# Two early weight sums in DRAM instead of one, and one subtraction instead of two, in a seven-product step of a down projection

## The chip, the core and the metric

The kernel runs on one core of one Trainium2 chip. The metric is device time in microseconds (us) of one execution, as the median of several runs. The core has five engines that matter here: TensorE (matmul; PE in the profile, with its weight loads as PEld), VectorE (DVE), ScalarE (ACT), GpSimd (POOL) and SyncE (SP), which only issues transfers. Sixteen DMA engines move the data. Transfers are put on queues by SyncE, GpSimd and, rarely, ScalarE; each of these engines works through its own instructions in order, so a transfer that has to wait holds the instructions behind it on that engine.

## What is computed

One layer of a hybrid decoder on 272 tokens (16 of them prepended and dropped at the end): a mixed retention and mLSTM part, and then a gated feed-forward part with a causal convolution. Only the last part is touched by the change:

```python
h = h + mix
u = rmsnorm(h, norm_ffn)
up = causal_dwconv(u @ w_up, ffn_conv_w, ffn_conv_b)      # 2048 -> 2 x 5632
gate, val = jnp.split(up, [FFN_DIM], axis=-1)
h = h + (jax.nn.silu(gate) * val) @ w_down                # 5632 -> 2048
...
h = rmsnorm(h, norm_final)
```

All inputs are float32. The kernel multiplies with float32 accuracy on a faster, shorter type: each operand x is split into hi, x rounded to that type (a copy on ScalarE), and lo = x - hi (a subtraction on VectorE), and each product is the sum of three matmuls, hi*hi, hi*lo and lo*hi.

## The kernel before

**Stages.** The input projection and the two kinds of heads run first, then the output projection. The feed-forward part then runs in two halves over the 5632 inner columns (`for half in range(2)`, line 724). Each half has an up projection (22 inner tiles, two products each, lines 749 to 790) and a down projection for its inner columns (lines 897 to 938).

**The down projection of a half.** The output's 2048 columns are four blocks of 512, taken in pairs: b = 0 with 1, then b = 2 with 3. For each pair the half's 22 inner tiles are taken two at a time, in 11 steps q. A *plain* step (q in PLAIN: 0, 4, 9, 10) loads the weights of block b and of block b + 1 with `load_w` (line 115) and multiplies all of its 2 x 2 x 2 tiles: eight products. A *fast* step (q in FAST: 1, 2, 3, 5, 6, 7, 8) treats its two inner tiles, two row tiles and two column blocks as a 2 x 2 by 2 x 2 product of tiles, and computes it with seven products instead of eight, after Strassen and Winograd: some products take sums of left tiles (S1 to S4, made on GpSimd in lines 782 to 785) and sums of weight tiles. The function `seven` (line 812) does one such step. In the very last pair the fast steps 7 and 8 are plain, so there are 7 + 7 + 7 + 5 = 26 fast steps in all.

**The weights of a fast step.** Four weight tiles, 128 x 512 each: B11, B12, B21 and B22, where the first index is the inner tile within the step and the second the column block within the pair. Their order in DRAM is fixed on the host in `a["wd7"]` (line 1007): B12, B11, B22, B21. The seven products need B11, B22, B21 as they are and four sums:

- t1 = B11 - B12, t2 = B22 + t1, t2 - B11 and B21 - t2.

**The early sum.** t2 is made ahead of time, during the up projection. An `Early` object (line 704) loads three tiles of a unit into a borrowed buffer (`home`) on GpSimd's queue (line 715), two projections later forms t2 there with two 128x512 operations on VectorE (lines 720 and 721), and stores t2 to a DRAM tile `kept` on GpSimd's queue (line 722). In the first half the homes of the first nine units are `x5[1:4]`; the last five use `left[0]`, `left[1]`, `x5[1:4]`, `left[0]`, `left[1]` in this order. `left[0]` and `left[1]` are also the two buffers into which the fast steps load their weights in turn.

**A fast step in `seven`.** SyncE loads t2 from `kept` (line 820, 256 KB) and B11, B22, B21 (line 821, 768 KB) into `raw`, one of the two `left` buffers. VectorE forms ta = t2 - (B11, B22), two tiles at once, of which the second is t1 again (line 824), and tb = B21 - t2, one tile (line 825). ta and tb lie in slots of the ring `wraw`, which has four slots of two tiles and also takes the weights that `load_w` loads: a later load waits until the slot's last reader is done. Then four groups of weights, three of two tiles and one of one, are split with `split` (line 743: a ScalarE copy in line 744, a VectorE subtraction in line 746) into the rings `whi` and `wlo` of five slots each, and multiplied (lines 839, 840 and 842).

**Order.** The instructions are written in the order of the loops; a planner puts them into each engine's queue by a timeline that it simulates. The trace shows the order that came of it.

Of the kernel before, what the change touches and what calls it, by code (L numbers as in the profile page):

```python
# [10 lines left out]
F32 = mybir.dt.float32  # L11
# [5 lines left out]
P = 128  # L17
# [66 lines left out]
def trunk(ctx: ExitStack, tc: tile.TileContext, io, out: bass.AP):  # L84
# [619 lines left out]
    class Early:  # L704


        def __init__(self, b, q, home, after):

            self.home, self.age = home, 0
            self.kept = dram.tile([P, 512], F32, name=f"kept{b}_{q % NQD}", bufs=1)  # L710

            if after is not None:
                after = nc.gpsimd.tensor_tensor(out=pace, in0=after[:, 0:1], in1=after[:, 0:1], op=ALU.add)
            with tc.issue_after(after.ins) if after else nullcontext():
                nc.gpsimd.dma_start(home, io["wd7"][b // 2, q][:, 0:3, :])

        def finish(self, after):
            t = self.home[:, 0, :]
            with tc.issue_after(after.ins):
                nc.vector.tensor_tensor(out=t, in0=self.home[:, 1, :], in1=t, op=ALU.subtract)  # L720
            nc.vector.tensor_tensor(out=t, in0=self.home[:, 2, :], in1=t, op=ALU.add)
            nc.gpsimd.dma_start(self.kept, t)

    for half in range(2):
        units = [(b, q) for b in (0, 2) for q in FAST if (half, b) != (1, 2) or q not in BOTH]
# [23 lines left out]
        for jj in range(NHF):  # L749
# [20 lines left out]
            if q in PLAIN:  # L770
                k = 2 * PLAIN.index(q) + i
                copied, parted = split(mh[:, k, :], ml[:, k, :], gt)
            elif i == 0:
                f = FAST.index(q)
                even = gt
                copied, parted = split(sh[:, f, A11, :], sl[:, f, A11, :], gt[:, 0:P])
            else:
                e11, e21, e12, e22 = even[:, 0:P], even[:, P:], gt[:, 0:P], gt[:, P:]
                if half == 1 and q in BOTH:
                    split(*(a[:, BOTH.index(q), :] for a in a21), e21)  # L780
                sums = x_tile(0).rearrange("p (a t) -> p a t", a=4)
                nc.gpsimd.tensor_tensor(out=sums[:, S1, :], in0=e21, in1=e22, op=ALU.add)
                nc.gpsimd.tensor_tensor(out=sums[:, S3, :], in0=e11, in1=e21, op=ALU.subtract)
                nc.gpsimd.tensor_tensor(out=sums[:, S2, :], in0=sums[:, S1, :], in1=e11, op=ALU.subtract)
                nc.gpsimd.tensor_tensor(out=sums[:, S4, :], in0=e12, in1=sums[:, S2, :], op=ALU.subtract)
                split(sh[:, f, A12:, :], sl[:, f, A12:, :], gt.rearrange("p (a t) -> p a t", a=2))
                copied, parted = split(sh[:, f, 0:4, :], sl[:, f, 0:4, :], sums)
# [24 lines left out]
        def seven(b, q, cs, ps, first, last, after, norm):  # L812
# [4 lines left out]
            raw = left[turn]  # L817
            turn = 1 - turn

            nc.sync.dma_start(raw[:, 0, :], early[b, q])  # L820
            nc.sync.dma_start(raw[:, 1:4, :], io["wd7"][b // 2, half * NQD + q][:, 1:4, :])
            ta, tb = (wpool.tile([P, 2, 512], F32, name="wraw", bufs=4) for _ in range(2))

            nc.vector.tensor_tensor(out=ta, in0=raw[:, 0:1, :].to_broadcast([P, 2, 512]), in1=raw[:, 1:3, :], op=ALU.subtract)  # L824
            nc.vector.tensor_tensor(out=tb[:, 0, :], in0=raw[:, 3, :], in1=raw[:, 0, :], op=ALU.subtract)
            copied = None
            for w, to in (
                (raw[:, 2:4, :], ((S4, cs[0, 1], False, False), (A12, cs[0, 0], False, False))),
                (raw[:, 0:2, :], ((S2, ps[2], first, last), (A11, ps[0], first, last))),
                (ta, ((S3, ps[1], first, last), (S1, ps[3], first, last))),  # L830
                (tb[:, 0:1, :], ((A22, cs[1, 0], False, False),)),
            ):
                hi = wpool.tile([P, 2, 512], F32R, name="whi", bufs=5)
                lo = wpool.tile([P, 2, 512], F32R, name="wlo", bufs=5)
                n = len(to)
                with tc.issue_after(after.ins) if first and after else nullcontext():
                    copied, _ = split(hi[:, :n, :], lo[:, :n, :], w)
                for i, (m, o, begin, _) in enumerate(to):
                    nc.tensor.matmul(o, sh[:, f, m, :], hi[:, i, :], start=begin, stop=False)  # L839
                    nc.tensor.matmul(o, sl[:, f, m, :], hi[:, i, :], start=False, stop=False)  # L840
                for i, (m, o, _, end) in enumerate(to):
                    nc.tensor.matmul(o, sh[:, f, m, :], lo[:, i, :], start=False, stop=end)  # L842
            if norm:

                with tc.issue_after(copied.ins):
                    for g in norm:
                        squares(*g)
                reached = nc.gpsimd.tensor_tensor(out=junk[:, 0:1], in0=tb[:, 0, 0:1], in1=tb[:, 0, 0:1], op=ALU.add)
                with tc.issue_after(reached.ins):
                    for tt, _, c0, c1 in norm:  # L850
                        times_gain(tt, c0, c1)
# [124 lines left out]
def _layout(x, meta_tokens, norm_mix, w_in, mlstm_conv_w, mlstm_conv_b, mlstm_b_i, mlstm_b_f,  # L976
# [27 lines left out]
    a["wd"] = np.ascontiguousarray(w_down[0].reshape(NF // 2, 2, P, 4, 512).transpose(3, 0, 2, 1, 4))  # L1004

    pairs = a["wd"].reshape(2, 2, NF // 2, P, 2, 512)
    a["wd7"] = np.ascontiguousarray(np.stack([pairs[:, 1, :, :, 0], pairs[:, 0, :, :, 0], pairs[:, 1, :, :, 1], pairs[:, 0, :, :, 1]], 3))

    def colmajor(v):
        return v.reshape(-1, P).T  # L1010
# [38 lines left out]
```

## Time and profile before

| | |
|---|---|
| timed runs | 1211.92, 1212.79, 1213.15 us; median 1212.79 |
| span of the profiled execution | 1210.4 us, from its first to its last instruction; its own device time is not recorded, and the median of the timed runs is 2.4 us above the span |
| busy over the span | TensorE 99%, its weight loads 95%, VectorE 80%, ScalarE 59%, GpSimd 14% |
| granted TensorE clock, mean | 0.998 of full speed |
| DMA | 263.27 MB, mean 218 GB/s |
| line 824, 128x1024 sum | 26 times, median 1218 ns |
| line 825, 128x512 sum | 26 times, median 684 ns |
| line 820, load of the kept sum | 26 times, 256 KB, median 2.6 us to landing |
| line 821, load of the three tiles | 26 times, 768 KB, median 4.5 us to landing |
| line 722, store of the kept sum | 14 times from `x5`, median 4.5 us, and 12 times from `left` (called hT), median 4.8 us |

In the trace's rows L is a line of the kernel. A row of a group says out<-in by the program's names: `wraw<-hT` is a sum that is read from `left`, since `left` is a view of the tile hT, and `x` is the tile x5. `in_wd` names both weight tensors of the down projection. Time in brackets is the idle time of the engine ahead of the instruction, with what released it.

### The profile page before, as it was taken

What the parts mean: (1) busy time and instruction counts of PE and PEld (TensorE: products, weight loads), DVE (VectorE), ACT (ScalarE), POOL (GpSimd) and SP (SyncE); (2) the same over time, 40 slices, a digit from 0 to 9 for tenths busy, and PEclk for the clock granted to TensorE, in tenths of its full rate; (3) what the DMA queues carried; (4) which work ended last, traced back from release to release, by engine and by line L of the source; (5) the groups of instructions that cost most, each with busy time, mean ns of one, the idle gap of its engine ahead of it and who ended that gap; (6) DMA issues with size and microseconds to landing.
All of it is one profiled execution on the core that took longest, in us unless ns stands there. A gap on an engine that the chain in (4) does not pass through costs nothing.

```text
span 1210.4 us, 22758 instructions
## 1 busy us (share of the span) xinstructions
PE 1198.6 (99%) x8956; PEld 1155.6 (95%) x8956; DVE 970.1 (80%) x1444; ACT 708.5 (59%) x963; POOL 165.1 (14%) x228
## 2 busy tenths in 40 slices
PE   9999999999999999999999999999999999999997
PEld 9999999999999999999999997788999999998886
DVE  8877778766775767789888879996798778789897
ACT  8657646656556656555555546665555555556674
POOL 0100001111110211021122210202022112100232
PEclk9999999999999999999999999999999999999999
DMA  8765555656564655766766775959777677755956
GB/s 277 265 220 160 166 189 171 199 175 189 181 193 141 208 178 176 248 220 208 246 225 209 270 268 202 261 200 272 275 252 261 216 245 239 259 177 208 286 179 185
DMA packets 83004, 263.27 MB, mean 218 GB/s; under 512 B 14672, under 2 KB 18896, under 8 KB 82768
## 3 DMA queue, kind: packets, MB, share of 16 engines
q1 hardware_dynamic: 71952, 223.85, 56.4%
q0 software_dynamic: 10368, 37.11, 10.0%
q8 instruction: 70, 1.15, 0.4%
q10 hardware_dynamic: 576, 0.85, 0.2%
q14 instruction: 38, 0.31, 0.1%
HBM read 243.42 MB, written 11.27 MB: 210 GB/s over the span
## 4 chain that ended last, share of the span: by engine, by line
PE 92%; DMA 4%; DVE 2%; issue 1%; ACT 0%; SPq 0%; DVEq 0%; POOL 0%; ACTq 0%; POOLq 0%
PE mmps L130 25%; PE mmps L131 25%; PE mmps L133 24%; PE atps L807 3%; PE atps L808 3%; PE atps L810 2%; PE mmps L842 2%; PE mmps L839 1%; PE mmps L840 1%; PE atps L842 1%; PE atps L840 1%; PE atps L839 1%; DMA wraw<-in_wd 1%; DMA hT<-in_wd 1%; DVE wlo L746 1%
## 5 line engine op out<-in xcount | busy, mean ns | idle before, releaser
L121 ACT CAST whi<-wraw 128x1024 fp32r<-128x1024 f32 x352 | 368.7, 1049 | 316.6 <-PE mmps L131 216.9
L123 DVE TENSOR_TENSOR wlo<-wraw,whi 128x1024 fp32r<-128x1024 f32 x352 | 433.1, 1232 | 71.9 <-ACT whi L121 69.6
L130 PE MATMUL mmps<-uh,whi 128*128 128x258 f32 x1408 | 346.7, 283 | 0.0
L131 PE MATMUL mmps<-ul,whi 128*128 128x258 f32 x1408 | 346.6, 283 | 0.0
L131 PEld LDWEIGHTS mmps<-ul,whi 128*128 128x128 f32 x1408 | 266.6, 189 | 0.1
L130 PEld LDWEIGHTS mmps<-uh,whi 128*128 128x128 f32 x1408 | 266.4, 189 | 0.1
L130 PE MATMUL mmps<-xh,whi 128*128 128x272 f32 (+2 forms) x864 | 219.9, 288 | 0.0
L131 PE MATMUL mmps<-xl,whi 128*128 128x272 f32 (+2 forms) x864 | 218.4, 286 | 0.0
L133 PE MATMUL mmps<-uh,wlo 128*128 128x258 f32 x1408 | 199.0, 283 | 0.0
L133 PEld LDWEIGHTS mmps<-uh,wlo 128*128 128x128 f32 x1408 | 181.3, 189 | 0.0
L131 PEld LDWEIGHTS mmps<-xl,whi 128*128 128x128 f32 x864 | 163.0, 189 | 0.0
L130 PEld LDWEIGHTS mmps<-xh,whi 128*128 128x128 f32 x864 | 162.7, 188 | 0.1
L133 PE MATMUL mmps<-xh,wlo 128*128 128x272 f32 (+2 forms) x864 | 126.8, 286 | 0.0
L133 PEld LDWEIGHTS mmps<-xh,wlo 128*128 128x128 f32 x864 | 114.4, 188 | 0.0
L633 DVE TENSOR_TENSOR cu<-mmps,rstd 128x258 f32<-128x258 f32 x88 | 37.3, 424 | 47.6 <-PE mmps L133 47.1
L746 DVE TENSOR_TENSOR wlo<-hT,whi 128x1024 fp32r<-128x1024 f32 x52 | 62.8, 1236 | 5.6 <-ACT whi L744 5.0
L744 ACT CAST whi<-hT 128x1024 fp32r<-128x1024 f32 x52 | 53.3, 1051 | 23.4 <-DMA hT<-in_wd 5.6
L131 PE MATMUL mmps<-mixl,whi 128*128 128x258 f32 x256 | 63.0, 283 | 0.0
L130 PE MATMUL mmps<-mixh,whi 128*128 128x258 f32 x256 | 62.4, 283 | 0.0
L744 ACT CAST whi<-wraw 128x1024 fp32r<-128x1024 f32 (+1 forms) x52 | 42.1, 835 | 18.5 <-DVE wraw L824 4.8
L807 PE MATMUL atps<-whi,mh 128*128 128x512 f32 (+1 forms) x132 | 50.9, 387 | 2.0 <-ACT whi L121 2.0
L746 DVE TENSOR_TENSOR wlo<-wraw,whi 128x1024 fp32r<-128x1024 f32 (+1 forms) x52 | 51.4, 1014 | 0.8 <-PE mmps L842 0.2
(276 smaller groups left out, 1704.4 us busy)
## 6 DMA issues: line engine op xcount, KB each, us to landing
wraw<-in_wu SPq DMA_DIRECT2D x176, 512.0 KB, 4.4
wraw<-in_wi SPq DMA_DIRECT2D x108, 512.0 KB, 4.2
hT<-in_wd SPq DMA_DIRECT2D x26, 768.0 KB, 4.5
wraw<-in_wd SPq DMA_DIRECT2D x36, 512.0 KB, 5.1
wraw<-in_wo SPq DMA_DIRECT2D x32, 512.0 KB, 3.8
x<-in_wd POOLq DMA_DIRECT2D x14, 768.0 KB, 7.6
hT<-in_wd POOLq DMA_DIRECT2D x12, 768.0 KB, 6.4
hn<-x POOLq DMA_DIRECT2D x27, 256.0 KB, 7.8
```

The source lines that it names most:

```text
L121: nc.scalar.copy(hi, raw)
L123: nc.vector.tensor_tensor(out=lo, in0=raw, in1=hi.bitcast(F32), op=ALU.subtract)
L130: nc.tensor.matmul(ps, hi[:, k, :], xh(kk), start=kk == first, stop=False)
L131: nc.tensor.matmul(ps, hi[:, k, :], xl(kk), start=False, stop=False)
L133: nc.tensor.matmul(ps, lo[:, k, :], xh(kk), start=False, stop=kk == last)
L633: evacuated = nc.vector.tensor_tensor(out=u, in0=ps[:, :NQ], in1=rstd2, op=ALU.mult)
L744: copied = nc.scalar.copy(hi, x)
L746: return copied, nc.vector.tensor_tensor(out=lo, in0=x, in1=hi.bitcast(F32), op=ALU.subtract)
L807: nc.tensor.matmul(ps, ah[i], hi[:, i, cols], start=first and i == 0, stop=False)
L808: nc.tensor.matmul(ps, al[i], hi[:, i, cols], start=False, stop=False)
L810: nc.tensor.matmul(ps, ah[i], lo[:, i, cols], start=False, stop=last and i == 1)
L842: nc.tensor.matmul(o, sh[:, f, m, :], lo[:, i, :], start=False, stop=end)
```

## The change

Both sums t1 and t2 are kept in DRAM. To that end the host stacks the four tiles in another order (B12, B22, B11, B21); `finish` leaves t1 in the first tile of the home and t2 in the second, with the same two operations, and stores both. A fast step loads t1 and t2 (512 KB), B11 and B21 (512 KB), both into `raw`, and B22 (256 KB) into a slot of the ring `wraw`, as a third transfer. One 128x1024 operation forms (B11, B21) - t2; the first of its two tiles has the other sign than before, which the left sum S3 takes back (e21 - e11 instead of e11 - e21). The four groups of weights are now (B11, B21), (t1, t2), B22 alone, and ta; the single tile comes third and not last.

```diff
--- before.py
+++ after.py
@@ -707,7 +707,7 @@
         def __init__(self, b, q, home, after):
 
             self.home, self.age = home, 0
-            self.kept = dram.tile([P, 512], F32, name=f"kept{b}_{q % NQD}", bufs=1)
+            self.kept = dram.tile([P, 2, 512], F32, name=f"kept{b}_{q % NQD}", bufs=1)
 
             if after is not None:
                 after = nc.gpsimd.tensor_tensor(out=pace, in0=after[:, 0:1], in1=after[:, 0:1], op=ALU.add)
@@ -715,11 +715,11 @@
                 nc.gpsimd.dma_start(home, io["wd7"][b // 2, q][:, 0:3, :])
 
         def finish(self, after):
-            t = self.home[:, 0, :]
+            t1, t2, b11 = (self.home[:, i, :] for i in range(3))
             with tc.issue_after(after.ins):
-                nc.vector.tensor_tensor(out=t, in0=self.home[:, 1, :], in1=t, op=ALU.subtract)
-            nc.vector.tensor_tensor(out=t, in0=self.home[:, 2, :], in1=t, op=ALU.add)
-            nc.gpsimd.dma_start(self.kept, t)
+                nc.vector.tensor_tensor(out=t1, in0=b11, in1=t1, op=ALU.subtract)
+            nc.vector.tensor_tensor(out=t2, in0=t2, in1=t1, op=ALU.add)
+            nc.gpsimd.dma_start(self.kept, self.home[:, 0:2, :])
 
     for half in range(2):
         units = [(b, q) for b in (0, 2) for q in FAST if (half, b) != (1, 2) or q not in BOTH]
@@ -780,7 +780,7 @@
                     split(*(a[:, BOTH.index(q), :] for a in a21), e21)
                 sums = x_tile(0).rearrange("p (a t) -> p a t", a=4)
                 nc.gpsimd.tensor_tensor(out=sums[:, S1, :], in0=e21, in1=e22, op=ALU.add)
-                nc.gpsimd.tensor_tensor(out=sums[:, S3, :], in0=e11, in1=e21, op=ALU.subtract)
+                nc.gpsimd.tensor_tensor(out=sums[:, S3, :], in0=e21, in1=e11, op=ALU.subtract)
                 nc.gpsimd.tensor_tensor(out=sums[:, S2, :], in0=sums[:, S1, :], in1=e11, op=ALU.subtract)
                 nc.gpsimd.tensor_tensor(out=sums[:, S4, :], in0=e12, in1=sums[:, S2, :], op=ALU.subtract)
                 split(sh[:, f, A12:, :], sl[:, f, A12:, :], gt.rearrange("p (a t) -> p a t", a=2))
@@ -817,18 +817,19 @@
             raw = left[turn]
             turn = 1 - turn
 
-            nc.sync.dma_start(raw[:, 0, :], early[b, q])
-            nc.sync.dma_start(raw[:, 1:4, :], io["wd7"][b // 2, half * NQD + q][:, 1:4, :])
-            ta, tb = (wpool.tile([P, 2, 512], F32, name="wraw", bufs=4) for _ in range(2))
-
-            nc.vector.tensor_tensor(out=ta, in0=raw[:, 0:1, :].to_broadcast([P, 2, 512]), in1=raw[:, 1:3, :], op=ALU.subtract)
-            nc.vector.tensor_tensor(out=tb[:, 0, :], in0=raw[:, 3, :], in1=raw[:, 0, :], op=ALU.subtract)
+            w = io["wd7"][b // 2, half * NQD + q]
+            nc.sync.dma_start(raw[:, 0:2, :], early[b, q])
+            nc.sync.dma_start(raw[:, 2:4, :], w[:, 2:4, :])
+            b22, ta = (wpool.tile([P, 2, 512], F32, name="wraw", bufs=4) for _ in range(2))
+            nc.sync.dma_start(b22[:, 0, :], w[:, 1, :])
+
+            nc.vector.tensor_tensor(out=ta, in0=raw[:, 2:4, :], in1=raw[:, 1:2, :].to_broadcast([P, 2, 512]), op=ALU.subtract)
             copied = None
             for w, to in (
-                (raw[:, 2:4, :], ((S4, cs[0, 1], False, False), (A12, cs[0, 0], False, False))),
-                (raw[:, 0:2, :], ((S2, ps[2], first, last), (A11, ps[0], first, last))),
-                (ta, ((S3, ps[1], first, last), (S1, ps[3], first, last))),
-                (tb[:, 0:1, :], ((A22, cs[1, 0], False, False),)),
+                (raw[:, 2:4, :], ((A11, ps[0], first, last), (A12, cs[0, 0], False, False))),
+                (raw[:, 0:2, :], ((S1, ps[3], first, last), (S2, ps[2], first, last))),
+                (b22[:, 0:1, :], ((S4, cs[0, 1], False, False),)),
+                (ta, ((S3, ps[1], first, last), (A22, cs[1, 0], False, False))),
             ):
                 hi = wpool.tile([P, 2, 512], F32R, name="whi", bufs=5)
                 lo = wpool.tile([P, 2, 512], F32R, name="wlo", bufs=5)
@@ -845,7 +846,7 @@
                 with tc.issue_after(copied.ins):
                     for g in norm:
                         squares(*g)
-                reached = nc.gpsimd.tensor_tensor(out=junk[:, 0:1], in0=tb[:, 0, 0:1], in1=tb[:, 0, 0:1], op=ALU.add)
+                reached = nc.gpsimd.tensor_tensor(out=junk[:, 0:1], in0=ta[:, 0, 0:1], in1=ta[:, 0, 0:1], op=ALU.add)
                 with tc.issue_after(reached.ins):
                     for tt, _, c0, c1 in norm:
                         times_gain(tt, c0, c1)
@@ -1004,7 +1005,7 @@
     a["wd"] = np.ascontiguousarray(w_down[0].reshape(NF // 2, 2, P, 4, 512).transpose(3, 0, 2, 1, 4))
 
     pairs = a["wd"].reshape(2, 2, NF // 2, P, 2, 512)
-    a["wd7"] = np.ascontiguousarray(np.stack([pairs[:, 1, :, :, 0], pairs[:, 0, :, :, 0], pairs[:, 1, :, :, 1], pairs[:, 0, :, :, 1]], 3))
+    a["wd7"] = np.ascontiguousarray(np.stack([pairs[:, 1, :, :, 0], pairs[:, 1, :, :, 1], pairs[:, 0, :, :, 0], pairs[:, 0, :, :, 1]], 3))
 
     def colmajor(v):
         return v.reshape(-1, P).T
```

## The prediction

> **What bounds the kernel now.** I read the page's first part first: how busy each engine is.
>
> ```profile
> span 1210.4 us, 22758 instructions
> PE 1198.6 (99%) x8956; PEld 1155.6 (95%) x8956; DVE 970.1 (80%) x1444; ACT 708.5 (59%) x963; POOL 165.1 (14%) x228
> ```
>
> TensorE is the bound. The change leaves every matmul as it is, so it can win only where TensorE waits for what the change touches. Next, the view of stages, cut at the edges of the fast steps. Behind each stretch and its length stand the busy time and the instructions of TensorE's matmuls, its weight loads, VectorE, ScalarE and GpSimd, then the granted clock, the DMA share and GB/s.
>
> ```profile
> 390.00:720.00 330.00, 330.00 (x2741) 329.94 (x2740) 267.03 (x387) 179.48 (x244) 58.56 (x85) 1.00 0.67 223
> 725.70:740.80 15.10, 14.21 (x62) 11.04 (x60) 15.10 (x18) 9.01 (x11) 0.00 (x0) 1.00 0.61 211
> 746.10:767.00 20.90, 19.66 (x86) 15.78 (x85) 20.10 (x21) 11.30 (x14) 0.00 (x0) 1.00 0.64 220
> 784.30:836.00 51.70, 51.70 (x233) 42.67 (x232) 47.29 (x50) 31.66 (x36) 4.38 (x5) 1.00 0.69 221
> 836.00:1091.00 255.00, 255.00 (x2110) 254.66 (x2109) 200.85 (x301) 139.42 (x189) 40.54 (x68) 1.00 0.73 244
> 1091.00:1199.00 108.00, 108.00 (x485) 89.05 (x484) 98.49 (x103) 69.12 (x86) 23.06 (x21) 1.00 0.68 215
> ```
>
> The 26 changed steps lie in four blocks. In three of them (784 to 836 and both in 1091 to 1199) TensorE is busy without a gap at a granted clock of 1.00, although VectorE is nearly full there too. Only the first block (fast steps 1, 2, 3 at 725.7 to 740.8 and 5 to 8 at 746.1 to 767.0) loses time, in two places. TensorE's timeline gives their size:
>
> ```profile
> 725.70 0.39 PE L839 MATMUL atps<-whi,sh 128*128 128x512 f32 x1
> 725.93 0.39 PE L840 MATMUL atps<-whi,sl 128*128 128x512 f32 x1
> ...
> 727.07 0.39 PE L839 MATMUL mmps<-whi,sh 128*128 128x512 f32 x1
> ...
> 738.51 0.63 PE L842 MATMUL atps<-wlo,sh 128*128 128x512 f32 x2
> 739.26 0.73 PE L842 MATMUL mmps<-wlo,sh 128*128 128x512 f32 x2
> 740.76 0.50 PE L807 MATMUL atps<-whi,mh 128*128 128x512 f32 x1 [0.76 <-ACT whi L121]
> 741.10 0.40 PE L808 MATMUL atps<-whi,ml 128*128 128x512 f32 x1
> ...
> 765.14 0.62 PE L842 MATMUL mmps<-wlo,sh 128*128 128x512 f32 x2
> 767.04 0.50 PE L807 MATMUL atps<-whi,mh 128*128 128x512 f32 x1 [1.28 <-ACT whi L121]
> 767.37 0.39 PE L808 MATMUL atps<-whi,ml 128*128 128x512 f32 x1
> ```
>
> A busy share hides part of it: 512-column matmuls start 0.23 us apart but are drawn 0.39 long. By starts, the first stall loses 0.29 (738.97 to 739.26) + 1.04 (739.72 to 740.76) + 0.11 (0.34 instead of 0.23) = 1.44 us. The second loses 1.44 (765.60 to 767.04) + 0.10 = 1.54 us. **Together 2.98 us, 0.25% of the span: no more than that is to be had.** What stands behind them is in the chain in order of time (start, length, what):
>
> ```profile
> 692.60 7.90 DMA x<-in_wd
> ...
> 704.77 6.17 DMA hT<-in_wd
> ...
> 712.95 5.21 DMA kept<-hT
> ...
> 718.18 5.09 DMA hT<-kept
> ...
> 723.29 0.69 DVE wraw L824
> ...
> 733.05 1.23 DVE wlo L746
> ...
> 734.29 5.27 DMA wraw<-in_wd
> ...
> 758.64 1.22 DVE wlo L746
> ...
> 759.88 5.96 DMA wraw<-in_wd
> ```
>
> Both stalls have one shape. The weights of the plain step after the fast ones (step 4, step 9) need a slot of the four-deep raw weight ring, which a fast step's sum holds until VectorE has split it; only then is the load issued (734.29, 759.88). The first stall has a longer root: VectorE starts the first fast step at 723.29, held by the early sum's way out to DRAM and back (712.95, 718.18), because the last early units use the very buffers the fast steps load into.
>
> **The change, part by part.** *VectorE loses L825.*
>
> ```profile
> 723.29 1.23 DVE L824 TENSOR_TENSOR wraw<-hT 128x1024 f32<-128x1024 f32 x1 [2.48 <-DMA hT<-kept]
> 724.44 0.68 DVE L825 TENSOR_TENSOR wraw<-hT 128x512 f32<-128x512 f32 x1
> 725.04 0.48 DVE L637 SCALAR_TENSOR_TENSOR vt<-cu,par,vt 128x256 f32<-128x256 f32 x1
> ```
>
> Each step forms its two sums in one 128x1024 operation, the form L824 has already; the 128x512 one goes. Successive starts (724.44 to 725.04) price it at 0.60 us, 26 x 0.60 = 15.6 us of VectorE. Where VectorE is not what ends TensorE's wait this is worth nothing. Between 723.29 and the release at 734.27 two L825 lie on the path: 1.20. The Trainium skill (VectorE: DVE Perf Modes, The DRAIN you can't avoid) says that the next operation does not start before the pipe is empty, which would price it at its 0.68 us and the two at 1.36; the rows show starts 0.08 before the end of the one ahead, so they decide.
>
> *The ring's release moves.* Now the slot that step 4's first load takes is held by step 2's 128x512 weight (b22), not by its 128x1024 sum. If b22's split (0.68 us, 0.60 by starts) stands where the sum's (1.22, 1.14 by starts) did, the release is 0.54 earlier. Together 1.74 us off the path to the first stall.
>
> *The kept sum doubles,* 256 to 512 KB out, and 256 to 512 KB back, 26 times. In most units nothing waits: the store is read again tens of us later and TensorE is gapless. For the last units of the first half it lies on the chain above. The nearest rows are the issues by line (KB each, median us to landing), GpSimd's first and last of the three stores ahead, the stages around them, and the cast of the kept sum:
>
> ```profile
> hT<-in_wd SPq DMA_DIRECT2D x26, 768.0 KB, 4.5
> hT<-in_wd POOLq DMA_DIRECT2D x12, 768.0 KB, 6.4
> hT<-kept SPq DMA_DIRECT2D x26, 256.0 KB, 2.6
> kept<-hT POOLq DMA_DIRECT2D x12, 256.0 KB, 4.8
> ...
> 693.63 0.55 POOL L722 DMA_DIRECT2D kept<-hT  x1 [0.46 <-DVE hT L721]
> 702.58 0.54 POOL L722 DMA_DIRECT2D kept<-x  x1 [3.77 <-DVE x L721]
> ...
> 690.00:700.00 10.00, 10.00 (x85) 10.00 (x84) 9.75 (x16) 5.83 (x9) 2.11 (x4) 1.00 1.01 388
> 700.00:712.00 12.00, 12.00 (x102) 12.00 (x101) 9.98 (x17) 6.41 (x9) 2.46 (x5) 1.00 0.89 333
> ...
> 723.35 1.06 ACT L744 CAST whi<-hT 128x1024 fp32r<-128x1024 f32 x1 [1.90 <-DMA hT<-kept]
> ```
>
> Store: (6.4 - 4.8)/2 = 0.8 us for 256 KB more. Read: (4.5 - 2.6)/2 = 0.95. And the DMA engines are full at 690 to 700 and nearly full to 712, where the three kept stores ahead carry 0.75 MB more: at 388 GB/s 256 KB takes 0.68 us, and I count one such delay for the early load of 692.60, which VectorE waits for and which so sets off that of 704.77, and one for the latter. **VectorE starts the first fast step 0.68 + 0.68 + 0.8 + 0.95 = 3.1 us later.** The lower bound is the two transfers alone at full rate, 1.35. The upper one doubles both transfers (5.21 + 5.09) and charges all three stores, 12.3. I take 3.1, from the rows of the same tiles and queues. TensorE doesn't feel all of it at once: the cast of the kept sum ended at 724.41 and its first matmul started 2.66 later, at 727.07; what is left over goes into the same first stall, not on top of it. The Trainium skill (DMA: Bandwidth & Descriptors, Anatomy of one DMA) fits a transfer as 2.0 us and its bytes at 436 GB/s; 256 KB more would cost 0.60, the delay would be 2.4 and the sum below 0.7 lower. No run here shows a 512 KB store yet.
>
> *Loads.* The step's 1.0 MB in two issues become 1.25 MB in three. The third, b22, waits on SyncE's queue for a ring slot two steps back; behind it stand the next step's loads, whose buffer comes free later than that, so nothing more is held. DMA share is 0.61 and 0.64 there, and what is needed first (w rows, kept sums) is 1.0 MB as before. I put it at nothing; if it pushed the plain loads behind it, it would cost 0.68 each. POOL's and SP's instruction counts otherwise stay: one issue (0.33 us) more per step on an idle SP. The swapped operands, the sign of one product's left side and the new product order cost nothing: the same operations in the same sizes, ScalarE at 9.01 of 15.10.
>
> *Extra traffic under the up projection:* TensorE is gapless at 390 to 720 (330.00 of 330.00), through the full DMA at 690 to 700 as well. I price it at nothing; if that cover were gone, 3 x 0.68 us.
>
> **The sum.** First stall: 1.44 + 3.1 - 1.74 = 2.8, so +1.36. Second stall: three L825 (steps 5 to 7) and the 0.54 of the release, 2.34 us off the path to the 759.88 issue, against 1.54 lost: gone, -1.54. Net -0.2: 1210.2 us of span. The timed median lies 1212.79 - 1210.4 = 2.4 above the span of the profiled execution; that stays. **1212.6 us.** With the delay between 1.35 and 5.0 this case alone runs from 1210.9 to 1214.5.
>
> **Rivals.**
> 1. *Both stalls go.* If the store and read grow by hardly anything (under 0.3 us in all), 1.74 exceeds 1.44 and the whole 2.98 is won: 1209.8. For it: a transfer's time is mostly constant in these rows. Against: the ring and the 388 GB/s.
> 2. *Slower: the kept path's trip through DRAM.* Place: the last early unit before the first fast step. With 12.3 us of delay, 1212.8 + 12.3 - 1.74 - 1.54 = 1221.8. It passes the 0.2% that a measurement of this kernel can tell from no change (2.4 us) once the delay exceeds 5.7. For it: 256 KB took 5.09 us where 2.6 is the median, so this stage is already congested. Against: the store uses as many rows, only longer.
> 3. *The second stall stays.* Step 9's load stands in SP's queue behind the next block's first raw loads (1.0 MB either way), and if these, not VectorE, set it, the 1.54 is not won: 1214.1. For it: its 5.96 us against 5.27 for the other. Against: VectorE was busy 20.10 of 20.90 there.
>
> That the change does not do what it says I leave out: it removes an instruction that is in the trace 26 times.
>
> **Chances.** Likeliest 0.56, both stalls gone 0.10, slower 0.20, second stall stays 0.14. Faster by over 0.2% (under 1210.4): the first rival, 0.10. Slower by over 0.2% (above 1215.2): the second, 0.20. Within: 0.56 + 0.14 = 0.70. The range runs from 1210.4, leaving out most of the first rival, to 1216.0, leaving out a bit over half of the second.
>
> **What would show it.** No 128x512 sum on VectorE, 26 fewer instructions; the kept store and read of the last early units at about 6.0 and 6.0 us, and the first sum of the first fast step near 726.4 instead of 723.29; a first stall of 2 to 3 us where TensorE goes to step 4's plain weights; none before step 9; no gap in the other three blocks. Wrong would be: the first sum no later than 724 (rival 1), later than 729 (rival 2), gaps in a block that had none, or a store ahead of the fast steps so reordered that the first stall has another root.

## The result and the profile after

The changed kernel is **slower**: median 1216.88 us (1215.3 to 1224.24, six runs) beside 1212.53 us of the kernel before, ratio 1.0052 (95% interval 1.0035 to 1.0069). The ratios on record aren't quotients of the medians (that would be 1.0036 here, and 1.0053 for the means). In a second measurement, on chip 1 (called the second chip below; the first one's number isn't on record), it was 1219.25 beside 1214.67 us, ratio 1.0037 (1.0023 to 1.0051). The forecast was 1212.6 us in a range up to 1216.0. The first two lines of the page of after:

```profile
span 1221.0 us, 22810 instructions
...
PE 1203.0 (99%) x8956; PEld 1157.2 (95%) x8956; DVE 955.8 (78%) x1418; ACT 709.1 (58%) x963; POOL 166.2 (14%) x228
```

VectorE has lost 26 operations and 14.3 us of work (970.1 before), as it should, and the span is 10.6 us longer. The profiled run (1222.77 us) and one more (1224.24) lie about 5 us or more above the other four (1215.30 to 1217.79), so this trace shows more loss than the median run has; the second chip's trace (1220.49 us, median 1219.25) is nearer to it. Where TensorE's time went is counted as in the prediction: from the starts of neighbouring matmuls, what exceeds the usual distance (0.23 us at 512 columns). Blocks are the stretches with seven-product steps; the up projection between them loses nothing in the kernels of this table.

| TensorE's loss, us | first block (700 to 784) | second (784 to 850) | third and fourth (from 1091) | sum |
|---|---|---|---|---|
| before | 2.98 | 0 | 0 | 2.98 |
| after | 5.68 | 2.75 | 4.24 | 12.7 |
| after, second chip | 3.88 | 2.07 | 3.80 | 9.8 |

Of the 10.6 us of span 9.7 are here; 0.65 stands on TensorE already 8 us after the start, where nothing was changed. More than half of the 9.7 is in blocks that were gapless. The view of TensorE's waits in after (who waited for whom; us in all, times, longest):

```profile
PE atps L807 <- ACT x L932: 2.8, 2, 2.4
PE mmps L840 <- ACT whi L744: 2.4, 1, 2.4
PE mmps L843 <- DVE wlo L746: 1.4, 1, 1.4
...
PE atps L807 <- ACT whi L121: 1.1, 2, 0.8
```

These are many places and not one: casts, splits, and ScalarE's copy L932, which stands behind a cast that waits for weights. What they have in common lies one engine upstream, as experiment 3 tests. The same view for VectorE, before and after:

```profile
DVE wraw L824 <- DMA hT<-kept: 2.5, 1, 2.5
```

```profile
DVE wraw L826 <- DMA hT<-kept: 15.2, 8, 3.2
```

**VectorE stands at the sum, L826, for the load of the kept sums: 15.2 us in eight waits, instead of 2.5 us in one.** On the second chip it was 14.4 us in eight. That is as much as the removed operation had saved. The transfers of after, from the view of DMA issues (KB each, median us from issue to landing):

```profile
hT<-in_wd SPq DMA_DIRECT2D x26, 512.0 KB, 4.3
hT<-kept SPq DMA_DIRECT2D x26, 512.0 KB, 4.8
...
hT<-in_wd POOLq DMA_DIRECT2D x12, 768.0 KB, 7.5
kept<-x POOLq DMA_DIRECT2D x14, 512.0 KB, 6.1
...
wraw<-in_wd SPq DMA_DIRECT2D x26, 256.0 KB, 4.8
kept<-hT POOLq DMA_DIRECT2D x12, 512.0 KB, 6.2
```

The kept load lands 4.8 us after its issue; it was 2.6. What this does to a step is seen in VectorE's timeline in the second block of after on the second chip (start, length, what; idle time ahead and what ended it in brackets):

```profile
809.02 1.23 DVE L826 TENSOR_TENSOR wraw<-hT 128x1024 f32<-128x1024 f32 x1 [1.61 <-DMA hT<-kept]
810.16 2.35 DVE L746 TENSOR_TENSOR wlo<-hT,whi 128x1024 fp32r<-128x1024 f32 x2
812.43 1.82 DVE L746 TENSOR_TENSOR wlo<-wraw,whi 128x512 fp32r<-128x512 f32 x2
814.17 1.22 DVE L746 TENSOR_TENSOR wlo<-hT,whi 128x1024 fp32r<-128x1024 f32 x1
816.91 1.23 DVE L826 TENSOR_TENSOR wraw<-hT 128x1024 f32<-128x1024 f32 x1 [1.52 <-DMA hT<-kept]
818.05 1.22 DVE L746 TENSOR_TENSOR wlo<-hT,whi 128x1024 fp32r<-128x1024 f32 x1
```

and in SyncE's queue, the same stretch:

```profile
803.43 0.33 SPq L822 DMA_DIRECT2D hT<-in_wd  x1
804.57 0.33 SPq L821 DMA_DIRECT2D hT<-kept  x1
806.30 0.33 SPq L824 DMA_DIRECT2D wraw<-in_wd  x1
811.41 0.33 SPq L822 DMA_DIRECT2D hT<-in_wd  x1
812.54 0.33 SPq L821 DMA_DIRECT2D hT<-kept  x1
```

Both sums start about 4.4 us after the issue of their kept load (804.57 to 809.02, 812.54 to 816.91), as soon as it has landed. What stands behind them are splits of the step *before*, which have their data: the one at 818.05 (its cast was done at 812.5, in ScalarE's timeline), for which TensorE lost 0.8 us at 818.3. And it is a loop: the splits at 810.16 free the buffer for the next loads, which go out as each of them ends (811.41 and 812.54); these set the next sum. (The step's third load, b22 at 806.30, waits for a slot of its ring on the same queue, but doesn't hold these: SyncE issued them within 0.05 us of the splits' ends, and in 20 of the 26 steps it stood waiting for such a split before the weight load, 49.0 us in all.) So 7.9 us pass from this sum to the next. The short lead isn't new. In the kernel before 9 of the 26 sums start less than 6 us after the issue of their kept load, in after 10 of 26; but there the load took 2.6 us and, but for the first step, left 1.5 to 3.1 to spare, and here it takes what there is.

**The first steps** come late too. VectorE's rows of after, of the last early units and the first sum:

```profile
716.28 0.69 DVE L720 TENSOR_TENSOR hT<-hT 128x512 f32<-128x512 f32 x1
...
729.12 1.23 DVE L826 TENSOR_TENSOR wraw<-hT 128x1024 f32<-128x1024 f32 x1 [3.15 <-DMA hT<-kept]
```

and GpSimd's:

```profile
706.84 0.57 POOL L715 DMA_DIRECT2D hT<-in_wd  x1 [0.28 <-issue]
...
708.95 0.57 POOL L715 DMA_DIRECT2D hT<-in_wd  x1 [0.88 <-DMA kept<-hT]
718.21 0.54 POOL L722 DMA_DIRECT2D kept<-hT  x1 [8.69 <-DVE hT L721]
```

This store (of an early unit further on) empties the buffer into which the first fast step loads its own sums, stored long before: SyncE issued that kept load at 723.84, as the store landed. So the first sum is 5.83 us later (723.29 before): the early load goes out 2.07 later (706.84, not 704.77; 0.65 of it is the shift of the whole trace), 9.44 us pass to the operation that takes it instead of 6.19 (L720 at 710.96 before), the store takes 5.63 to the issue of the kept load instead of 5.23, and from there to the sum it is 5.28 instead of 5.11. The doubled transfers themselves are 0.6 us of it. Of the 9.44 the early load took 7.41 (6.17 before); for the other 2.0 its operation stood behind a split of plain weights on VectorE. On the second chip the first sum started at 727.38.

### The profile page after: what moved, and what is told of

Same layout as the page of the kernel before. It is cut to its first block, busy times and chain, and to the rows that moved or that the text cites. A ratio compares the mean times of both kernels' runs of the same rounds, so it can differ in the third digit from the quotient of the medians.

```text
span 1221.0 us, 22810 instructions
## 1 busy us (share of the span) xinstructions
PE 1203.0 (99%) x8956; PEld 1157.2 (95%) x8956; DVE 955.8 (78%) x1418; ACT 709.1 (58%) x963; POOL 166.2 (14%) x228
## 5 line engine op out<-in xcount | busy, mean ns | idle before, releaser
L744 ACT CAST whi<-wraw 128x512 fp32r<-128x512 f32 (+1 forms) x52 | 42.5, 837 | 17.3 <-DMA wraw<-in_wd 3.9
L746 DVE TENSOR_TENSOR wlo<-wraw,whi 128x512 fp32r<-128x512 f32 (+1 forms) x52 | 50.1, 996 | 2.7 <-ACT whi L744 1.9
```

The source lines that it names most:

```text
L744: copied = nc.scalar.copy(hi, x)
L746: return copied, nc.vector.tensor_tensor(out=lo, in0=x, in1=hi.bitcast(F32), op=ALU.subtract)
```

## The experiments

Ratios are to the kernel before on the same chip, with 95% intervals; a loss is TensorE's from 690 us on. A changed line also moves others, since the planner sets the queues anew; where that spoils a reading, it is said.

**1. The changed kernel again**, and both kernels with their last early units begun sooner:

```diff
-            begins = [2 + 4 * i for i in range(9)] + [36, 37, 38, 40, 41]
-            homes = 9 * [homes[2]] + homes + homes
+            begins = [2 + 3 * i for i in range(12)] + [36, 37]
+            homes = 12 * [homes[2]] + homes[:2]
```

> The changed kernel once more, for a second trace on the same chip as the others. Both theories expect 1215 to 1218 us. The trip theory (the last early units' way through DRAM holds the first fast step of the first half) expects that TensorE's first wait near 727 us recurs with about the same length in this trace; the traffic theory (256 KB more read in each fast step makes the loads behind it late) expects the waits near 775 to 782, 820 to 830 and 1145 to 1156 us to recur.

> The changed kernel with the early units of the first half started every 3 projections and the last two at 36 and 37 instead of 40 and 41, so that no kept store lies close ahead of the first fast step. Trip theory: the first wait goes, 2.5 to 4 us are won, 1213 us or less. Traffic theory: the waits of the later blocks stay and at most 1 us is won, 1216 us.

> The kernel before with the early units of the first half started every 3 projections and the last two at 36 and 37. Trip theory: the first stall's root goes and 0.4 to 1.4 us are won, 1211.1 to 1212.1 us. Traffic theory: no change, 1212.5.

The edit did what it was to do: the first sum started at 720.31 in the changed kernel (729.12 and 727.38 without the edit), and at 717.74 in the one before. Both were slower: 1.0089 (1.0070 to 1.0108) and 1.0062 (1.0045 to 1.0079). TensorE lost 14.5 and 9.2 us, mostly waiting for splits and casts, 3.2 us of the first in the up projection. The edit does harm of its own, in both kernels, so these ratios alone don't tell what the first trip through DRAM costs. But with the first sum 7 to 9 us earlier the later blocks of the changed kernel still lost 4.7 us (5.9 and 7.0 without the edit): the trip isn't the cause of these. Why the units do harm there was not followed up.

**2. The kernel before with its 128x512 sum on GpSimd**, so that VectorE loses the operation and no byte moves:

```diff
-            nc.vector.tensor_tensor(out=tb[:, 0, :], in0=raw[:, 3, :], ...)
+            nc.gpsimd.tensor_tensor(out=tb[:, 0, :], in0=raw[:, 3, :], ...)
```

> The kernel before with its 128x512 sum (line 825) formed on GpSimd: VectorE is freed of it as in the change, with no traffic added. If VectorE's share is worth what the prediction said for a start that is not late, up to 2.98 us are won (1209.6 to 1211.5). If a later sum or the shared memory port eats it, 1212.5 or more.

1.0184 (1.0171 to 1.0197). The operation has a median of 2.2 us there, with up to 7.8, and 0.68 on VectorE; the splits behind it come late in every block. It tells nothing of VectorE's saving.

**3. The sum behind the first split.** One operation changes places on VectorE:

```diff
-            nc.vector.tensor_tensor(out=ta, ...)
...
-                    copied, _ = split(hi[:, :n, :], lo[:, :n, :], w)
+                    copied, lower = split(hi[:, :n, :], lo[:, :n, :], w)
+                if parted is None:
+                    parted = lower
+                    with tc.issue_after(parted.ins):
+                        nc.vector.tensor_tensor(out=ta, ...)
```

> The changed kernel, with the sum of a seven-product step put behind the first wlo operation of the step on VectorE, so that the split which needs only the weights is no longer queued behind the wait for the kept sums. Nothing else is changed. Theory of the queue (the 512 KB load of the kept sums lands 4 to 5 us after its half of the buffer is free, not 2.6 as the 256 KB load did; VectorE stands at the sum for it, 15 us in all, with splits behind it): VectorE waits under 8 us for kept sums, the three later blocks of seven-product steps lose under 3 us of TensorE instead of 5.9, ratio to before 0.999 to 1.002. Theory of the traffic (6.8 MB more written and 6.8 MB more read make all transfers later): the ratio stays at 1.0035 to 1.005. Theory of the trip (only the first kept sum's way through DRAM counts): the first block loses 4 us as now, the other blocks as now.

> The changed kernel with the sum behind the first wlo operation of its step once more, in more rounds and beside the kernel before with the same move. Theory of the queue: ratio 0.997 to 1.000 as before, one stall of over 0.5 us left (near 740 us, step 4's plain weights), VectorE's waits for kept sums under 4 us in all. Theory that the first such run was a lucky one: 1.001 to 1.004.

> A single look at the same kernel again for its waits: VectorE's waits for kept sums under 4 us in all, TensorE losses after 700 us under 2.5 us.

> The changed kernel with its sum behind the first wlo operation, beside the one with the longer wlo operation on the same chip: 0.997 to 1.000.

Ratios 0.9984 (0.9972 to 0.9995), 0.9987 (0.9978 to 0.9997) and 0.9984 (0.9968 to 1.0001); the single run gave 1208.96 us. SyncE issues the loads in the order of the changed kernel. The losses are 1.5, 1.5, 0.3 and 4.2 us in place of 9.8 and 12.7. VectorE's waits and timeline in the second of these runs, the issue of the kept load for the last sum shown, and the median to landing:

```profile
DVE wraw L841 <- DMA hT<-kept: 2.0, 1, 2.0
```

```profile
804.00 1.22 DVE L746 TENSOR_TENSOR wlo<-hT,whi 128x1024 fp32r<-128x1024 f32 x1
805.13 1.22 DVE L841 TENSOR_TENSOR wraw<-hT 128x1024 f32<-128x1024 f32 x1
806.27 1.22 DVE L746 TENSOR_TENSOR wlo<-hT,whi 128x1024 fp32r<-128x1024 f32 x1
807.40 1.82 DVE L746 TENSOR_TENSOR wlo<-wraw,whi 128x512 fp32r<-128x512 f32 x2
809.14 1.22 DVE L746 TENSOR_TENSOR wlo<-hT,whi 128x1024 fp32r<-128x1024 f32 x1
810.28 1.22 DVE L841 TENSOR_TENSOR wraw<-hT 128x1024 f32<-128x1024 f32 x1
```

```profile
802.37 0.33 SPq L821 DMA_DIRECT2D hT<-kept  x1
```

```profile
hT<-kept SPq DMA_DIRECT2D x26, 512.0 KB, 5.1
```

There is no gap, although the kept load takes 5.1 us here (4.8 in after) and as many bytes move. The sum now stands behind a split of its own step, so all splits of the step before are ahead of it, and the loop is cut: a step takes 5.1 us, and the kept load of the sum at 810.28 was issued at 802.37, 7.9 us ahead of it. No sum, or one of 26, starts less than 6 us after that issue. The first sum of all started at 724.8, 725.0, 723.9 and 727.5 us in the four profiles; with the last the first block lost 1.3 us at 727, as in after on the second chip, so part of what the first block won may be an earlier first sum. The later blocks have no such trip, and lost 0 to 0.8 us in all instead of 5.9 and 7.0. **The sum's wait at the head of VectorE's queue, with ready splits behind it, is the cause of most of the loss, and this is a version that beats both kernels**, the one before by 0.15% (the medians are 1.8, 0.3 and 1.7 us apart, and the third interval reaches 1.0001) and the changed one by some 0.5% (each measured beside the kernel before, on different chips). It is the wait together with its place that is shown: in experiments 5 and 7 the waits fall to 5.9 and 5.3 us while the sum stays where it was, and the time is not won back.

**4. The same move in the kernel before**, with both its sums, so that it isn't the move alone that is measured.

> The kernel before with both its sums put behind the first wlo operation of the step on VectorE, as was done with the changed kernel's one sum. Theory of the queue (the move pays only where VectorE stood at the sum for the kept load, which here lands in 2.6 us and was waited for once, 2.5 us): TensorE loses as much as before, about 3 us, or a little more since the sums hold their slots of the ring longer; ratio 0.999 to 1.002. Rival, that the move alone makes any of these kernels faster and the change adds nothing to it: 0.997 to 0.999, the same as for the changed kernel with it.

1.0062 (1.0049 to 1.0075), worse than either theory had it; the loss is 8.3 us. Here the kept load lands in 2.7 us and VectorE had little to wait for, so the move has nothing to win. Its price is seen at the old second stall, in TensorE's timeline:

```profile
764.11 0.62 PE L845 MATMUL mmps<-wlo,sh 128*128 128x512 f32 x2
767.24 0.80 PE L807 MATMUL atps<-whi,mh 128*128 128x512 f32 x1 [2.50 <-ACT whi L121]
```

The plain step's weights come 2.7 us late, 1.4 in the kernel before. That the sums, formed later, hold their slots of the ring longer is the explanation expected; the run shows the stall, not its root. So the gain in 3 takes the change and the move together.

**5. VectorE's time given back.** First by writing one of the two sums a second time, in the changed kernel and in that of 3; then, in that of 3, by letting the split of the single tile b22 form both halves of its output (1.22 instead of 0.68 us, 0.54 more a step), which leaves the order of loads and operations as it was:

```diff
+            nc.vector.tensor_tensor(out=ta[:, 1, :], in0=raw[:, 3, :], in1=raw[:, 1, :], op=ALU.subtract)
```

```diff
+                    if n == 1:
+                        copied = nc.scalar.copy(hi[:, :1, :], w)
+                        nc.vector.tensor_tensor(out=lo, in0=w.to_broadcast([P, 2, 512]), in1=hi[:, :1, :]..., op=ALU.subtract)
...
```

> The changed kernel with one 128x512 operation more in each step (it writes again one of the two sums), which gives back to VectorE the 0.60 us a step that the change had saved. Theory of the queue: VectorE stood idle for 15 us before the sums, so that what was saved bought nothing, and giving it back costs little: ratio 1.003 to 1.006, the wait for kept sums falls from 15 us to under 8. Rival, that VectorE's time is on the path after the wait: 1.007 to 1.015.

> The changed kernel with its sum behind the first wlo operation, and one 128x512 operation more in each step (it writes one of the two sums again), so that VectorE works as long as in the kernel before. If the wait at the sum was all that counted, ratio 0.998 to 1.000 as without the operation. If VectorE's 0.60 us a step is on the path once the wait is gone, 1.002 to 1.007, as the kernel before with its sums at that place gave 1.0062.

> The changed kernel with its sum behind the first wlo operation, in which the wlo operation of the single tile b22 forms both halves of its output (128x1024, about 1.22 us, in place of 128x512, 0.68 us; the second half is not read). VectorE works 0.54 us a step longer, nearly what the change had saved (0.60), while the order of SP's loads and of VectorE's operations is that of the kernel without it. If the wait at the sum was all that made the changed kernel slow: 0.998 to 1.000, as without it. If VectorE's time is on the path: 26 steps by 0.54 are 14 us of work, of which some 8 steps stand on the path, 1.002 to 1.007.

The changed kernel with the second writing: 1.0075 (1.0050 to 1.0099), loss 9.4 us. The wait for kept sums fell to 5.9 us, as the theory of the queue had it, but the time didn't come back. The ratio lies in the rival's range, but its interval reaches into both; and three kept loads moved ahead of weight loads in SyncE's queue, and VectorE's order changed, so this run doesn't decide between them. The kernel of 3 with it: 1.0282 (1.0258 to 1.0305), and this says something else. The added operation came out behind two more splits, and ScalarE's cast of the sums waited for it, with the next step's casts behind:

```profile
830.77 0.61 ACT L744 CAST whi<-wraw 128x512 fp32r<-128x512 f32 x1
834.95 1.04 ACT L744 CAST whi<-wraw 128x1024 fp32r<-128x1024 f32 x1 [3.56 <-DVE wraw L842]
```

The longer split is the clean one: 1.0037 (1.0023 to 1.0050) beside 0.9984 without it on the same chip, the wait for kept sums still 2.0 us in one, the loss 11.2 us. 0.0053 of 1214.55 us is 6.4 us for 26 x 0.54 = 14 us of work: **once nothing makes VectorE wait, near half of what it saves reaches the end**. By the two intervals it is 4 to 9 us, from one pair of runs; and the products of the longer split also get their operand 0.54 us later, which this doesn't separate.

**6. The bytes alone, in the kernel before.** A store twice as wide (512 KB, the second half of no use); a second store of 256 KB instead; and one more load of 256 KB a step that nothing reads:

```diff
...
-            nc.gpsimd.dma_start(self.kept, t)
+            nc.gpsimd.dma_start(self.kept, self.home[:, 0:2, :])
...
```

```diff
...
+            nc.gpsimd.dma_start(self.spare, self.home[:, 1, :])
```

```diff
+            nc.sync.dma_start(tb[:, 1, :], io["wd7"][b // 2, half * NQD + q][:, 0, :])
```

> The kernel before, whose early units store 512 KB to DRAM (two tiles, the second of no use) while a step reads back 256 KB as before. Theory of the trip and of the early loads (the wider stores make the early loads of the units ahead later): the first kept sum comes 2 to 4 us later, the first block loses 3 to 5 us instead of 3.0, the other three none; ratio 1.000 to 1.002. Theory of the queue: the same, since the kept loads are 256 KB: the three later blocks stay gapless. Theory of the traffic: half of the extra bytes, ratio 1.002 to 1.003, with losses in the later blocks.

> The kernel before with a second store of 256 KB behind each early unit's store, to a place of its own in DRAM which nobody reads: the extra bytes written alone, with the loads in the order in which the kernel before issues them. Theory of the queue: the kept load stays 256 KB, VectorE waits for it under 4 us in all, ratio 0.999 to 1.002, losses in the first block alone. Theory of the traffic: 1.002 to 1.004, with stalls in the later blocks.

> The kernel before, with one more load of 256 KB in each seven-product step, into the half of a weight slot that the 128x512 sum leaves empty (nothing reads it): 1.25 MB in three tensors... of loads a step in place of 1.0, as in the changed kernel. Theory of the queue: the kept load stays 256 KB and VectorE waits for it once, 2.5 us, as before; the three later blocks stay gapless, ratio 1.000 to 1.001. Theory of the traffic: the later blocks lose 2 to 4 us of TensorE, ratio 1.002 to 1.004. Theory of the trip: no change in the later blocks, 1.000.

Ratios 1.0019 (1.0009 to 1.0028), 1.0024 (1.0014 to 1.0034) and 1.0017 (1.0007 to 1.0027). In the first, two kept loads also moved ahead of weight loads in SyncE's queue, and its largest stall, 1.9 us at 725.5, is a cast that waits for such weights; the second has the loads in the old order. VectorE's order of operations changed in all three. The first lost 7.0 us of TensorE. The losses of the second and third are 5.0 and 5.5 us against 2.98, nearly all in the first block (4.6 and 5.1); the later blocks lost 0.4 each, and the kept load landed in 2.7 and 2.8 us. So the bytes cost 2.0 and 2.5 us in these traces, in the first block, and none of the three makes the 15 us of waits for loads at the sum (4.0, 0.8 and 4.4 us). Added up, the second and third ratios come to 0.4%, as much as the changed kernel loses. That the bytes aren't the explanation is seen from the place, since the changed kernel lost 5.9 and 7.0 us in the later blocks, and from experiment 3, which moves all these bytes and loses 0.3 to 4.2 us.

**7. What makes the kept load late.** A third buffer for two steps of each block, so that loads can start sooner; a kept load of 256 KB behind the same weight load (one product takes other weights); and the products of the kept sums put first, so that their half of the buffer comes free first:

```diff
+            place = 0 if first else place + 1
+            if place in (2, 5):
+                raw = x5[:, 1:5, :]
...
```

```diff
-            nc.gpsimd.dma_start(self.kept, self.home[:, 0:2, :])
+            nc.gpsimd.dma_start(self.kept, t2)
...
-            nc.sync.dma_start(raw[:, 0:2, :], early[b, q])
+            nc.sync.dma_start(raw[:, 1, :], early[b, q])
+            nc.sync.dma_start(raw[:, 0, :], w[:, 0, :])
```

```diff
-                (raw[:, 2:4, :], ((A11, ps[0], first, last), (A12, cs[0, 0], False, False))),
                 (raw[:, 0:2, :], ((S1, ps[3], first, last), (S2, ps[2], first, last))),
+                (raw[:, 2:4, :], ((A11, ps[0], first, last), (A12, cs[0, 0], False, False))),
```

> The changed kernel, with a third buffer for the step's four tiles, used by the third and the sixth step of each block, so that the loads of these steps and of those behind them can start about a step earlier. Theory of the queue: the kept sums of the later steps are there before VectorE asks; VectorE waits under 5 us for them, the later blocks lose under 2 us of TensorE, ratio 0.998 to 1.002. Theory of the traffic: as many bytes, so 1.003 to 1.005. Theory of the trip: as the changed kernel in the first block, 1.002 to 1.005.

> The changed kernel in which an early unit stores only its second sum (256 KB) and a step loads that alone from it; the place of the first sum is filled with 256 KB of weights, which wait for nothing but the buffer (one of the seven products is then formed with other weights, so the output differs in that part). As many bytes are read, half as many stored. The sum needs only the 256 KB kept load. Theory of the queue: that load lands sooner after its issue than the 4.8 us of the 512 KB one, and VectorE's wait for it falls below 8 us, ratio 1.000 to 1.003. Theory of the bytes read: they are unchanged, so 1.003 to 1.005 and a wait of 12 to 16 us as now.

> The changed kernel with the products of the kept sums ahead of those of the step's two weight tiles, so that the kept half of the buffer comes free first and its load is issued ahead of the 512 KB weight load instead of behind it. The sum still stands at the head of the step on VectorE. If the kept load is late because of what stands ahead of it: it lands in 3 to 4 us after its issue instead of 4.8 to 5.0, but the sum needs the weight tiles too, which now land last, so VectorE waits at the sum for these instead (10 us or more in all, named as the load of weights), and the ratio stays at 1.002 to 1.006. If it is late because of its own size: it lands in 4.5 to 5 us as now and stays what the sum waits for. If only the order of the two loads mattered: ratio below 1.001 and waits at the sum under 5 us.

The third buffer cut VectorE's waits for kept sums to 5.3 us, and the ratio stayed at 1.0055 (1.0033 to 1.0077), where the theory of the queue had 0.998 to 1.002: it missed. TensorE then waited for plain weights (2.5 us at 740.6, 1.4 at 800.1) and splits. The narrow kept load is no better than the wide one: 1.0082 (1.0050 to 1.0115), with

```profile
DVE wraw L827 <- DMA hT<-kept: 12.9, 7, 3.2
```

```profile
hT<-kept SPq DMA_DIRECT2D x26, 256.0 KB, 4.1
```

The same 256 KB landed in 2.6 us in the kernel before. So its own size is little of what makes it late. With the kept load issued 1.1 us ahead of the weight load instead of behind it, it was 1.0092 (1.0066 to 1.0118), and VectorE's waits say

```profile
DVE wraw L826 <- DMA hT<-in_wd: 12.0, 7, 2.5
...
DVE wraw L826 <- DMA hT<-kept: 4.5, 2, 4.0
```

The wait has the other name and the same size. The medians to landing are 4.4 us for the kept load and 5.4 for the weights; they were 4.8 and 4.3. **Whichever of the two loads that the sum needs is issued last, the sum at the head of the step waits for it.** Which part of the time to landing is due to the two loads sharing the DMA engines, and which to what SyncE issues behind them, stays open.

## Why the prediction was wrong

- **TensorE as the bound and two stalls to win** held. The second stall is gone in after, as forecast; on the second chip 0.5 us of it is left at 767. The first, forecast at 2.8 us, shrank to 0.2 at 744, and on the second chip stayed at 1.7.
- **VectorE loses L825**: 15.6 us forecast, 14.3 measured in busy time. Its worth was seen too small: two operations on the path to the first stall and three on that to the second, where the longer split shows near half of all 26, but only with nothing to wait for.
- **The failing step is "Loads", "I put it at nothing"**, with the sentence that in most units nothing waits for the kept sum. I priced the doubled read at 0.95 us, on the path of the first step alone, and argued for the other 25 from the time at which the *store* is read and from TensorE being gapless. What counts is the read's issue, which hangs on the buffer, and its landing, 4.8 us instead of 2.6, against a sum that stands ahead of other steps' splits, with a lead under 6 us in a third of the steps, on an engine over 90% busy (VectorE had 47.29 of 51.70 us in the second block). The leads were in the trace of before; I didn't read them. The 15.2 us of waits in place of 2.5 come from there, with 2.75 and 4.24 us of TensorE lost in blocks that were to stay gapless. (The fit of the Trainium skill, DMA: Bandwidth & Descriptors, Anatomy of one DMA, is for a transfer that GpSimd issues, as the stores are, and as an estimate gives 0.60 us for 256 KB more; the medians of the stores grew by 1.4 and 1.6 here, from 4.8 to 6.2 and from 4.5 to 6.1, and that of the kept load, which SyncE issues, by 2.2.) My fallback of 0.68 us for a late plain load named the wrong queue: the one behind the wait is VectorE's.
- **The delay of the first sum**, forecast at 3.1 us, was 5.83 and 4.09. The terms were mis-sized against each other: store and read grew by 0.6 together in after, not 1.75; the early load, the operation behind it and the load's start took the rest (1.24, 2.0 and 2.07 against 0.68 and 0.68). The chain of the prediction also reads as one sum's way out and back. It is two: what SyncE loads at 718.18 is the first step's own sum, stored long before, and it waited for the buffer that the other unit's store (712.95) empties. The two still stand one behind the other, so the forecast's total is not changed by it. Nor did the rest flow into the first stall: it showed as a stall of its own at 727, 2.55 us, where TensorE reaches the products of the kept sums.
- **The sum** had -0.2 us of TensorE; it was +9.7 in after and +6.8 on the second chip.
- **The rivals.** The slower one had the sign but not the mechanism: its place was the first fast step, and moving that up by 7 to 9 us (experiment 1) made things worse; a late first sum costs the 1.3 to 2.6 us at 727, and is the lesser part. A first sum later than 729 and gaps in gapless blocks were both named as signs of error; the gaps came in both traces, the late sum in the first alone (729.12, and 727.38 on the second chip).
- **Extra traffic at nothing** was off by a little: the bytes stored and the bytes read cost about 0.2% each by themselves, in the first block.

## What to carry to other kernels

Where an operation waits for the last of several transfers, look at what is queued behind it on its engine, and let work that has its data go first: here one operation in another place turned a loss of 0.4 to 0.5% into a gain of 0.15%. A change that trades an engine's work for bytes must be priced at every step that waits for those bytes, by issue and landing against the time of need, and not only at the step that is late today. Time saved on a nearly full engine is worth something only if the engine does not spend it waiting.

## What the runs showed of the hardware

After some stalls TensorE comes back slow. In after, behind a stall that lost 2.55 us:

```profile
727.49 0.40 PE L843 MATMUL atps<-wlo,sh 128*128 128x512 f32 x1
730.28 0.79 PE L840 MATMUL mmps<-whi,sh 128*128 128x512 f32 x1 [2.38 <-ACT whi L744]
730.87 0.63 PE L841 MATMUL mmps<-whi,sl 128*128 128x512 f32 x1
731.29 0.63 PE L840 MATMUL mmps<-whi,sh 128*128 128x512 f32 x1
731.72 0.63 PE L841 MATMUL mmps<-whi,sl 128*128 128x512 f32 x1
```

The starts are 0.43 us apart, not 0.23, and the stages around them (start and end, length, busy time and count of TensorE, its weight loads, VectorE, ScalarE and GpSimd, then the granted clock, DMA share and GB/s) show a clock below 1.00:

```profile
728.00:732.00 4.00, 1.72 (x4) 1.44 (x5) 2.88 (x4) 2.82 (x4) 0.00 (x0) 0.77 0.76 231
732.00:736.00 4.00, 4.00 (x15) 3.17 (x15) 4.00 (x5) 4.00 (x5) 0.00 (x0) 0.80 0.83 282
```

That stall cost 1.6 us more than its length. In all traces of this case, between 690 and 1203 us, of 14 stalls that lost 1.96 to 3.44 us ten were followed by 5 to 12 such matmuls, and of four that lost 1.72 to 1.93 none. But one of 1.53 us, at 1151 in the second kernel of experiment 5, was followed by eight, so the length of a stall alone doesn't decide it. The Trainium skill (TensorE: Matmul & The Clock Gate, Part 1: The HAM clock gate) tells of a clock at half rate, 426.7 ns for 512 columns, after an idle window of about 3.4 us; the distance agrees with the 0.43, while most of the idle times here were well below that.
